# SSM units one tile earlier, RG-LRU scans at tiles 12 and 13, and a second buffer for pair sums in a hybrid recurrent decoder step

## The chip, the cores and the metric

The kernel runs on one core of a Trainium2 chip. The metric is device time in microseconds of one execution; the kernel before takes 869.88 us, the median of three runs (868.09 to 870.44).

## What is computed

One layer of a decoder trunk on 544 tokens (32 of a sample group, 512 of a prompt), in fp32:

```
z = x @ w_in                                  # 1024 -> 6144, split among branches and gates
A: h = RG-LRU scan(conv4(xa)); out_a = (h * gelu(ya)) @ proj_a
B: out_b = (sb * conv3(sc * sh)) @ proj_b
C: y = Re(C state) + D u, a diagonal complex SSM scan over us (32 groups x 64 states)
   zc = gelu(y); out_c = (zc * sigmoid(zc @ glu_w + glu_b)) @ proj_c
m = g0 * out_a + g1 * out_b + g2 * out_c      # g = sigmoid of the last 3072 columns of z
x = LN(ALPHA * x + m @ w_out)
x = LN(ALPHA * x + square(relu(x @ mlp_up)) @ mlp_down)
```

All new states (conv buffers, RG-LRU and SSM states) are outputs too.

## The kernel before, in words

Every large product is made of three matmuls on a high and a low part of each operand (`mm3`, L148): a weight block of 128x1024 comes from DRAM into a `raw` buffer (three of them), ACT rounds it into `wh` and DVE makes `wl = raw - wh`. Four pairs of `wh`/`wl` buffers (five from tile 28 on) stand between these splits and PE. Results go to a ring of four PSUM buffers named `big`; a matmul group on a buffer waits until the group's result of four before has been read out.

The program is written as a row of tiles, numbered by `ti`. Tiles 0 to 7 are the xa and ya columns of z, 8 to 11 sb, 12 to 19 sc and sh in turn (an odd tile ends with the short convolution, a dozen DVE instructions), 20 to 27 the second branch's merge (`merge_b`: 24 pairs of matmuls for the gate and 12 for the projection in each), 28 to 35 the first branch's (`merge7`). The third branch's merge, `w_out` with the first layer norm, the MLP and the second layer norm follow. After each tile `run_side(ti)` calls what was put at that number by `at(...)`.

So the SSM is laid between the tiles. It is cut into eight units of two state groups. For unit u, `ssm_a` (tile `UA[u]`) has PE transpose a small matrix, `ssm_b` (`UB[u]`) makes products whose results DVE multiplies by a rotation (`xx`, `xy`, `X`), scans (L526) and rotates back, POOL joining the two halves of the state `HP`, and `ssm_c` (`UC[u]`) has PE multiply them, the first half at L544 and the second at L545. PE takes its instructions in the order of the program: where `HP` isn't there, PE stands. The RG-LRU's coefficients, scans and outputs (`a_coef`, `a_scan`, `a_first`, `a_out`) are put at tiles in the same way and run on DVE.

A third piece is the paired product `pair7` (L886): seven products in place of eight, on sums of blocks. It needs sums of the weights (`add_pair`: four POOL additions of 128x512 into a buffer `sr`, then split by ACT into `wh` at L851 and by DVE into `wl` at L852) and sums of x (`t_sum`, or `t_make` in the MLP; split by `t_put` into `Tt`, ACT at L790 and DVE at L791). In the MLP `t_make` uses an `sr` buffer of the same pool too, and that pool has one buffer.

The order of instructions of each engine is made by a scheduler, by priorities and estimated costs; what it has put in a row is then executed in that order.

Of the kernel before, what the change touches and what calls it, by code (L numbers as in the profile page):

```python
# [11 lines left out]
F32 = mybir.dt.float32  # L12
# [7 lines left out]
NB, NS = 8, 4  # L20
# [13 lines left out]
RAHEAD = 2  # L34
W2 = 1
AH1 = 4
UA = [12, 14, 16, 18, 20, 22, 23, 25]
UB = [a + 1 for a in UA]
UC = [a + (2 if a > 18 else 3) for a in UA]
K4_FIRST = {"a": (3,), "c": ()}  # L40
# [24 lines left out]
def kernel(ctx: ExitStack, tc: tile.TileContext, I, O):  # L65
# [101 lines left out]
    xh = [stile(F32R, name="xh") for _ in range(2)]  # L167
    xl = [stile(F32R, name="xl") for _ in range(2)]
    cp = const.tile([128, NCP], F32, name="cp")
    gw = const.tile([128, 2, 4, 128], F32, name="gw")  # L170

    def C(n, a=0, b=None):
        o, w = CP[n]
# [199 lines left out]

    def params_af():
        mag, dn, cn, sn = (P[n] for n in ("mag", "dn", "cn", "sn"))
        A_r = const.tile([128, 16, 4], F32, name="A_r")
        A_i = const.tile([128, 16, 4], F32, name="A_i")
        F_r = const.tile([128, 16, 4], F32, name="F_r")
        F_i = const.tile([128, 16, 4], F32, name="F_i")
        u1, u2 = stemp(16), stemp(16)  # L380

        def cmul(orr, oi, ar, ai, br, bi):
            tt(G, u1, ar, br, MUL)
            tt(G, u2, ai, bi, MUL)
            tt(G, orr, u1, u2, SUB)
            tt(G, u1, ar, bi, MUL)
            tt(G, u2, ai, br, MUL)
            tt(G, oi, u1, u2, ADD)

        tt(G, A_r[:, :, 0], mag, cn[:, 0], MUL)  # L390
        tt(G, A_i[:, :, 0], mag, sn[:, 0], MUL)
        cmul(A_r[:, :, 1], A_i[:, :, 1], A_r[:, :, 0], A_i[:, :, 0], A_r[:, :, 0], A_i[:, :, 0])
        cmul(A_r[:, :, 2], A_i[:, :, 2], A_r[:, :, 1], A_i[:, :, 1], A_r[:, :, 0], A_i[:, :, 0])
        cmul(A_r[:, :, 3], A_i[:, :, 3], A_r[:, :, 1], A_i[:, :, 1], A_r[:, :, 1], A_i[:, :, 1])
        rho = ptile(16, "rho")
        tt(G, rho, mag, mag, MUL)
        tt(G, rho, rho, rho, MUL)
        nr = stemp(16)
        ts(G, nr, A_r[:, :, 0], 1.0, None, SUB)
        ni = A_i[:, :, 0]  # L400
        tt(G, u1, nr, C("are"), MUL)
        tt(G, u2, ni, C("aim"), MUL)
        tt(G, u1, u1, u2, ADD)
        tt(G, F_r[:, :, 3], u1, dn, MUL)
        tt(G, u1, ni, C("are"), MUL)
        tt(G, u2, nr, C("aim"), MUL)
        tt(G, u1, u1, u2, SUB)
        tt(G, F_i[:, :, 3], u1, dn, MUL)
        for s in range(3):
            cmul(F_r[:, :, s], F_i[:, :, s], F_r[:, :, 3], F_i[:, :, 3], A_r[:, :, 2 - s], A_i[:, :, 2 - s])  # L410
        P.update(A_r=A_r, A_i=A_i, F_r=F_r, F_i=F_i, rho=rho)
# [27 lines left out]
    MM = [s1.tile([128, 2, 128], F32, tag=f"M{i}", name="M") for i in range(2)]  # L439
    for M_z in MM:  # L440
        G.memset(M_z, 0.0)
    ssr = const.tile([128, 16, NB], F32, name="ssr")
    ssi = const.tile([128, 16, NB], F32, name="ssi")

    def ssm_load(u):
        bc = s1.tile([128, 2, 4, 32], F32, tag="bc", name="bc", bufs=2)
# [230 lines left out]
    side = {}  # L677
# [20 lines left out]
    for ct in range(4):  # L698
        at(2 * ct + 2, a_gate, ct)
        at(2 * ct + 3, a_rec, ct)  # L700
        at(10 + ct, a_coef, ct)
        at(14 + ct, a_scan, ct)
        at(18 + ct, a_out, ct)
    at(0, params_trig)
    at(0, etable)
    at(0, params_af)
    side[9].insert(0, (a_sqrt, ()))
    side[14].insert(0, (a_first, ()))
    at(UB[7], ssm_state)
    at(UC[7], lambda: x_load())  # L710


    ti = 0
# [64 lines left out]

    N1, N2 = slice(0, H2), slice(H2, T)
    X0 = [[t[i] for t in (xh, xl)] for i in range(2)]  # L780
    xq = []

    def x_load():
        for i in range(2):
# [9 lines left out]
    def t_sum(i):  # L794
# [1 line left out]
        d, e = ((a, N1), (a, N2), (b, N2), (b, N1))[i], ((a, N2), (b, N2), (b, N2), (b, N1))[i]  # L796
        f = (d, d, (a, N1), (b, N2))[i]
        d, e, f = (x[:, :, n] for x, n in (d, e, f))
        tt(G if i == 1 else V, d, e, f, SUB)

    def t_next():
        a, b = xq
# [212 lines left out]
    merge_b(bh, bl)  # L1015

    ph1.close()
    srp = ctx.enter_context(tc.tile_pool(name="srp", bufs=1))
    upp = ctx.enter_context(tc.tile_pool(name="upp", bufs=1))
    wst["wp2"] = ctx.enter_context(tc.tile_pool(name="wp2", bufs=W2))  # L1020
    base = cur[0]
# [24 lines left out]
    wq["free"] = [wst["wp2"]] * W2 + [wp] * 4  # L1046
    pump()
    wq["cap"] = 4 + W2
    for i in range(4):
        t_sum(i)  # L1050
    Tt0 = []
    merge7(AQ["ah"], AQ["al"], K4_FIRST["a"], (0,))
    for i in sorted(side):
        run_side(i)
# [448 lines left out]
```

## Time and profile before

| what | value |
| --- | --- |
| median of 3 runs | 869.88 us |
| profiled execution | 870.71 us, of which the span is 868.9 us |
| PE busy | 841.5 us (97%) |
| DVE busy | 621.6 us (72%) |
| ACT busy | 374.0 us (43%) |
| POOL busy | 337.0 us (39%) |

The span runs from the first to the last recorded instruction; the other 1.81 us of that execution lie around it. PE's idle time is 27.4 us, and it lies in few places: 4.6 us at the start, 7.5 us at the end, and the rest in waits that the rows below list.

### The profile page before, as it was taken

How to read it: one execution, taken by the hardware profiler on the slowest of the kernel's cores; microseconds unless marked ns; L12 is line 12 of the kernel's file. 1: busy time of each engine (PE TensorE's matmuls, PEld its weight loads, DVE VectorE, ACT ScalarE, POOL GpSimd, SP SyncE). 2: the span in 40 equal slices, each digit the busy share in tenths (PEclk: the TensorE clock that was granted, in tenths of full speed). 3: DMA queues.
4: the chain of work that ended last, by engine and by line, in shares of the span. 5: the costliest groups of instructions: out<-in, count | busy, mean ns of one | idle time of the engine just before them, and what ended most of it. 6: DMA issues, size and time to landing. Idle time of an engine off the chain costs nothing.

```text
span 868.9 us, 16015 instructions
## 1 busy us (share of the span) xinstructions
PE 841.5 (97%) x6516; PEld 831.0 (96%) x6516; DVE 621.6 (72%) x963; ACT 374.0 (43%) x616; POOL 337.0 (39%) x363
## 2 busy tenths in 40 slices
PE   7999999898999899999999999899999999999996
PEld 7999998898999899999998999899999999999996
DVE  6978969986446766898758787666565666655656
ACT  4453744334432434644437765444343434444310
POOL 1089957777537443633001130422222212122022
PEclk9999999999999999999999999999999999999999
DMA  8352141223125253233754543333232333333202
GB/s 304 120 135 85 50 127 32 80 61 98 34 70 191 71 149 97 73 98 98 249 170 143 160 134 98 112 107 97 79 100 90 98 97 98 98 97 126 93 9 96
DMA packets 31593, 93.99 MB, mean 108 GB/s; under 512 B 3424, under 2 KB 9952, under 8 KB 31136
## 3 DMA queue, kind: packets, MB, share of 16 engines
q1 hardware_dynamic: 31232, 91.92, 33.9%
q8 instruction: 51, 0.84, 0.4%
q0 software_dynamic: 288, 1.05, 0.3%
q14 instruction: 22, 0.18, 0.1%
HBM read 88.24 MB, written 2.49 MB: 104 GB/s over the span
## 4 chain that ended last, share of the span: by engine, by line
PE 78%; DVE 14%; issue 3%; ACT 3%; POOL 1%; DMA 1%; DVEq 0%; SPq 0%; ACTq 0%; POOLq 0%
PE big L148 50%; PE big L886 21%; PE big L1171 3%; DVE wl L117 1%; PE big L1330 1%; DVE Tt L791 1%; DVE X L526 1%; DVE wl L852 1%; DVE cacc L613 1%; DVE xx L240 1%; DVE xy L240 1%; DMA raw<-in_w_dram 1%; ACT wh L851 1%; DVE X L240 1%; PE big L1112 1%
## 5 line engine op out<-in xcount | busy, mean ns | idle before, releaser
L240 POOL TENSOR_TENSOR sr<-raw 128x512 f32<-128x512 f32 x38 | 61.0, 1626 | 242.9 <-DMA raw<-in_w_dram 192.9
L117 DVE TENSOR_TENSOR wl<-raw,wh 128x1024 fp32r<-128x1024 f32 x70 | 96.3, 1379 | 39.4 <-ACT wh L116 39.2
L886 PE MATMUL big<-Tt,wh 128*128 128x272 f32 x608 | 117.7, 290 | 5.7 <-DVE Tt L791 3.0
L148 PE MATMUL big<-xh,wh 128*128 128x272 f32 (+2 forms) x544 | 116.2, 295 | 5.1 <-DVE wh L203 4.6
L116 ACT CAST wh<-raw 128x1024 fp32r<-128x1024 f32 x70 | 73.1, 1048 | 105.5 <-PE big L148 61.1
L148 PE MATMUL big<-xl,wh 128*128 128x272 f32 (+2 forms) x544 | 114.0, 291 | 0.0
L148 PE MATMUL big<-xh,wl 128*128 128x272 f32 (+2 forms) x544 | 113.4, 290 | 0.0
L851 ACT CAST wh<-raw 128x1024 fp32r<-128x1024 f32 (+1 forms) x73 | 68.3, 937 | 94.5 <-PE big L148 49.7
L852 DVE TENSOR_TENSOR wl<-raw,wh 128x1024 fp32r<-128x1024 f32 (+1 forms) x73 | 92.4, 1267 | 17.6 <-ACT wh L851 16.6
L886 PEld LDWEIGHTS big<-Tt,wh 128*128 128x128 f32 x608 | 95.6, 188 | 7.4 <-DVE Tt L791 3.6
L148 PE MATMUL big<-fh,wh 128*128 128x272 f32 (+2 forms) x448 | 98.1, 289 | 0.0
L148 PE MATMUL big<-fh,wl 128*128 128x272 f32 (+2 forms) x448 | 97.9, 288 | 0.0
L148 PE MATMUL big<-fl,wh 128*128 128x272 f32 (+2 forms) x448 | 97.7, 288 | 0.0
L148 PEld LDWEIGHTS big<-xh,wh 128*128 128x128 f32 x544 | 86.5, 192 | 5.7 <-ACT xh L202 4.6
L886 PE MATMUL big<-Tt,wl 128*128 128x272 f32 x304 | 88.0, 290 | 0.8 <-DVE wl L852 0.8
L148 PEld LDWEIGHTS big<-xl,wh 128*128 128x128 f32 x544 | 86.3, 192 | 0.1
L148 PEld LDWEIGHTS big<-xh,wl 128*128 128x128 f32 x544 | 85.7, 191 | 0.0
L851 ACT CAST wh<-sr 128x1024 fp32r<-128x1024 f32 x38 | 39.7, 1046 | 79.7 <-POOL sr L240 60.9
L852 DVE TENSOR_TENSOR wl<-sr,wh 128x1024 fp32r<-128x1024 f32 x38 | 47.9, 1260 | 35.5 <-ACT wh L851 35.5
L148 PEld LDWEIGHTS big<-fh,wh 128*128 128x128 f32 x448 | 72.4, 188 | 0.0
L148 PEld LDWEIGHTS big<-fl,wh 128*128 128x128 f32 x448 | 72.4, 188 | 0.0
L148 PEld LDWEIGHTS big<-fh,wl 128*128 128x128 f32 x448 | 72.0, 189 | 0.0
(291 smaller groups left out, 2093.0 us busy)
## 6 DMA issues: line engine op xcount, KB each, us to landing
raw<-in_w_dram SPq DMA_DIRECT2D x147, 512.0 KB, 3.6
xq<-in_xT_dram SPq DMA_DIRECT2D x2, 1088.0 KB, 7.2
xraw<-in_xT_dram SPq DMA_DIRECT2D x3, 544.0 KB, 7.1
raw<-in_w_dram SPq DMA_DIRECT2D x3, 384.0 KB, 6.2
x<-in_xT_dram SPq DMA_DIRECT2D x2, 576.0 KB, 4.9
U<-us_t SPq DMA_DIRECT2D x16, 68.0 KB, 4.1
zc<-Y SPq DMA_DIRECT2D x16, 68.0 KB, 3.7
bc<-in_bc_dram SPq DMA_DIRECT2D x8, 128.0 KB, 2.2
```

The source lines that it names most:

```text
L116: S.copy(h, r)
L117: V.tensor_tensor(l, r, h.bitcast(F32), op=SUB)
L148: PE.matmul(out, w, x[:, a:b], start=first and oi == 0, stop=last and oi == 2)
L240: e.tensor_tensor(o, a, b, op=op)
L526: V.tensor_tensor_scan(X_[:, r, j], rb, X_[:, r, j], 0.0, op0=MUL, op1=ADD)
L613: V.scalar_tensor_tensor(acc, xp[:, k:568 + k], w(k), acc, op0=MUL, op1=ADD)
L791: V.tensor_tensor(d[:, 1], t, d[:, 0].bitcast(F32), op=SUB)
L851: S.copy(h[:, 0:n], src)
L852: V.tensor_tensor(l[:, 0:n], src, h[:, 0:n].bitcast(F32), op=SUB)
L886: PE.matmul(out, w[:, sl], y[:, k], start=k == 0 and oi == 0, stop=k == 3 and oi == 2)
L1112: PE.transpose(tp[0:n, ft // 4, o:o + 128], x1[ft // 4][:, ft % 4, c0:c1], ident)
L1171: PE.matmul(out, x, w[:, sl], start=first and kk == 0 and oi == 0, stop=kk == K - 1 and oi == 2)
```

## The change

The table `UA` is moved one tile forward, and two for units 5 and 7, and with it `UB` and `UC`: `UC` becomes 14, 16, 18, 20, 21, 22, 24, 25 instead of 15, 17, 19, 21, 22, 24, 25, 27. The coefficients and scans of the RG-LRU go from one channel block per tile (10 to 13, 14 to 17) to two per tile (10 and 11, 12 and 13). The load of x for tile 28's merge follows `UC[7]`; its four sums, which were made just ahead of that merge, are put at tile 26, and one of them goes from POOL to DVE; the first split of them is put at tile 27. The pool of `sr` has two buffers instead of one. Seven tables (`gw`, `A_r`, `A_i`, `F_r`, `F_i`, `ssr` and `ssi`) live in a pool that is given back before tile 28.

```diff
@@ -34,7 +34,7 @@
 RAHEAD = 2
 W2 = 1
 AH1 = 4
-UA = [12, 14, 16, 18, 20, 22, 23, 25]
+UA = [11, 13, 15, 17, 19, 20, 22, 23]
 UB = [a + 1 for a in UA]
 UC = [a + (2 if a > 18 else 3) for a in UA]
 K4_FIRST = {"a": (3,), "c": ()}
@@ -167,7 +167,7 @@
     xh = [stile(F32R, name="xh") for _ in range(2)]
     xl = [stile(F32R, name="xl") for _ in range(2)]
     cp = const.tile([128, NCP], F32, name="cp")
-    gw = const.tile([128, 2, 4, 128], F32, name="gw")
+    gw = s1.tile([128, 2, 4, 128], F32, tag="gw", name="gw")
 
     def C(n, a=0, b=None):
         o, w = CP[n]
@@ -373,10 +373,10 @@
 
     def params_af():
         mag, dn, cn, sn = (P[n] for n in ("mag", "dn", "cn", "sn"))
-        A_r = const.tile([128, 16, 4], F32, name="A_r")
-        A_i = const.tile([128, 16, 4], F32, name="A_i")
-        F_r = const.tile([128, 16, 4], F32, name="F_r")
-        F_i = const.tile([128, 16, 4], F32, name="F_i")
+        A_r = s1.tile([128, 16, 4], F32, tag="A_r", name="A_r")
+        A_i = s1.tile([128, 16, 4], F32, tag="A_i", name="A_i")
+        F_r = s1.tile([128, 16, 4], F32, tag="F_r", name="F_r")
+        F_i = s1.tile([128, 16, 4], F32, tag="F_i", name="F_i")
         u1, u2 = stemp(16), stemp(16)
 
         def cmul(orr, oi, ar, ai, br, bi):
@@ -439,8 +439,8 @@
     MM = [s1.tile([128, 2, 128], F32, tag=f"M{i}", name="M") for i in range(2)]
     for M_z in MM:
         G.memset(M_z, 0.0)
-    ssr = const.tile([128, 16, NB], F32, name="ssr")
-    ssi = const.tile([128, 16, NB], F32, name="ssi")
+    ssr = s1.tile([128, 16, NB], F32, tag="ssr", name="ssr")
+    ssi = s1.tile([128, 16, NB], F32, tag="ssi", name="ssi")
 
     def ssm_load(u):
         bc = s1.tile([128, 2, 4, 32], F32, tag="bc", name="bc", bufs=2)
@@ -698,16 +698,19 @@
     for ct in range(4):
         at(2 * ct + 2, a_gate, ct)
         at(2 * ct + 3, a_rec, ct)
-        at(10 + ct, a_coef, ct)
-        at(14 + ct, a_scan, ct)
+        at(10 + ct // 2, a_coef, ct)
+        at(12 + ct // 2, a_scan, ct)
         at(18 + ct, a_out, ct)
     at(0, params_trig)
     at(0, etable)
     at(0, params_af)
     side[9].insert(0, (a_sqrt, ()))
-    side[14].insert(0, (a_first, ()))
+    side[12].insert(0, (a_first, ()))
     at(UB[7], ssm_state)
     at(UC[7], lambda: x_load())
+    for i in range(4):
+        at(UC[7] + 1, lambda i=i: t_sum(i))
+    at(UC[7] + 2, lambda: t_next())
 
 
     ti = 0
@@ -778,7 +781,7 @@
 
     N1, N2 = slice(0, H2), slice(H2, T)
     X0 = [[t[i] for t in (xh, xl)] for i in range(2)]
-    xq = []
+    xq, Tt0 = [], []
 
     def x_load():
         for i in range(2):
@@ -796,7 +799,7 @@
         d, e = ((a, N1), (a, N2), (b, N2), (b, N1))[i], ((a, N2), (b, N2), (b, N2), (b, N1))[i]
         f = (d, d, (a, N1), (b, N2))[i]
         d, e, f = (x[:, :, n] for x, n in (d, e, f))
-        tt(G if i == 1 else V, d, e, f, SUB)
+        tt(V, d, e, f, SUB)
 
     def t_next():
         a, b = xq
@@ -1015,7 +1018,7 @@
     merge_b(bh, bl)
 
     ph1.close()
-    srp = ctx.enter_context(tc.tile_pool(name="srp", bufs=1))
+    srp = ctx.enter_context(tc.tile_pool(name="srp", bufs=2))
     upp = ctx.enter_context(tc.tile_pool(name="upp", bufs=1))
     wst["wp2"] = ctx.enter_context(tc.tile_pool(name="wp2", bufs=W2))
     base = cur[0]
@@ -1046,9 +1049,6 @@
     wq["free"] = [wst["wp2"]] * W2 + [wp] * 4
     pump()
     wq["cap"] = 4 + W2
-    for i in range(4):
-        t_sum(i)
-    Tt0 = []
     merge7(AQ["ah"], AQ["al"], K4_FIRST["a"], (0,))
     for i in sorted(side):
         run_side(i)
```

Three lines are added to the file, so a line of before such as L791 is L794 after.

DVE at the first SSM unit, before. `xx` and `xy` are the unit's rotations, `X` its scan, `vv` and `bacc` the short convolution, `bx` the RG-LRU scan:

```order
L240 TENSOR_TENSOR xx_1630<-big_1622,E_r_595 128x512
L765 SCALAR_TENSOR_TENSOR bacc_1613<-up_1606,cp_94,bacc_1613 128x560
L240 TENSOR_TENSOR xy_1631<-big_1622,E_i_596 128x512
L767 SCALAR_TENSOR_TENSOR vv_1616<-up_1606,cp_94,bacc_1613 128x32
L769 SCALAR_TENSOR_TENSOR vv_1616<-up_1606,cp_94,bacc_1613 128x512
L240 TENSOR_TENSOR X_1629<-xx_1630,xy_1631 128x256
L240 TENSOR_TENSOR vv_1616<-vv_1616,us_t_159 128x544
L240 TENSOR_TENSOR X_1629<-xx_1630,xy_1631 128x256
L526 SCALAR_TENSOR_TENSOR X_1629<-rho_666,X_1629 128x128 x4
L240 TENSOR_TENSOR tm_1716<-r_841,cp_94 128x32
L665 SCALAR_TENSOR_TENSOR bx_451<-r_841,bx_451 128x512
L240 TENSOR_TENSOR xx_1630<-X_1629,E_r_595 128x512
```

The same place after:

```order
L117 TENSOR_TENSOR wl_1607<-raw_1401,wh_1606 128x1024
L240 TENSOR_TENSOR big_1456<-big_1456,dq_1249 32x64
L240 TENSOR_TENSOR tm_1553<-r_841,cp_94 128x32
L665 SCALAR_TENSOR_TENSOR bx_451<-r_841,bx_451 128x512
L240 TENSOR_TENSOR bx_451<-tm_1553,bx_451 128x4x8
L240 TENSOR_TENSOR tm_1553<-r_841,bx_451 128x32
...
L662 COPY st_96<-bx_451 128x4x8
L240 TENSOR_TENSOR gy_452<-gy_452,bx_451 128x544
L665 SCALAR_TENSOR_TENSOR bx_451<-r_841,bx_451 128x512 x2
L240 TENSOR_TENSOR xx_1573<-big_1565,E_r_595 128x512
L240 TENSOR_TENSOR xy_1574<-big_1565,E_i_596 128x512
```

The RG-LRU's first steps and three of its four scans stood behind the unit's rotations and now stand ahead of them; the convolution stands behind.

DVE at the start of the first branch's merge, before. `Tt` is the split of a sum of x:

```order
L852 TENSOR_TENSOR wl_3506<-raw_3329,wh_3505 128x1024
L791 TENSOR_TENSOR Tt_3509<-xq_3269,Tt_3509 128x1088
L791 TENSOR_TENSOR Tt_3512<-xq_3271,Tt_3512 128x1088
L791 TENSOR_TENSOR Tt_3515<-xq_3269,Tt_3515 128x1088
L852 TENSOR_TENSOR wl_3560<-raw_3501,wh_3559 128x1024
```

And after:

```order
L855 TENSOR_TENSOR wl_3335<-raw_3317,wh_3334 128x1024
L794 TENSOR_TENSOR Tt_3277<-xq_3103,Tt_3277 128x1088
...
L855 TENSOR_TENSOR wl_3509<-raw_3332,wh_3508 128x1024
L794 TENSOR_TENSOR Tt_3512<-xq_3105,Tt_3512 128x1088
L794 TENSOR_TENSOR Tt_3515<-xq_3103,Tt_3515 128x1088
L855 TENSOR_TENSOR wl_3560<-raw_3504,wh_3559 128x1024
```

One of three splits in a row has gone ahead into the tile before.

ACT at the MLP's first paired product, before. `rl` is an output tile of the MLP's upper half leaving PSUM and `fh` its high part; `wh_6234` and `wh_6238` are the splits of the weight's pair sums `sr_6229`, and `sr_6194` is the buffer of `t_make`:

```order
L1226 CAST fh_5763<-rl_6105 128x256
L851 CAST wh_6225<-raw_6211 128x1024
L1224 ACTIVATE rl_6135<-big_6134 128x256
L1226 CAST fh_5763<-rl_6135 128x256
L1224 ACTIVATE rl_6165<-big_6164 128x256
L1226 CAST fh_5763<-rl_6165 128x256
L790 CAST Tt_6196<-sr_6194 128x1088
...
L790 CAST Tt_6208<-sr_6194 128x1088
L851 CAST wh_6234<-sr_6229 128x1024
L851 CAST wh_6238<-sr_6229 128x1024
L851 CAST wh_6294<-raw_6217 128x512
```

And after:

```order
L1226 CAST fh_5763<-rl_6105 128x256
L854 CAST wh_6238<-sr_6229 128x1024
L854 CAST wh_6225<-raw_6211 128x1024
L1224 ACTIVATE rl_6135<-big_6134 128x256
L1226 CAST fh_5763<-rl_6135 128x256
L1224 ACTIVATE rl_6165<-big_6164 128x256
L854 CAST wh_6234<-sr_6229 128x1024
L1226 CAST fh_5763<-rl_6165 128x256
L793 CAST Tt_6196<-sr_6194 128x1088
L793 CAST Tt_6200<-sr_6194 128x1088
L854 CAST wh_6294<-raw_6217 128x512
```

The split `wh_6238` of the pair sums has moved ahead of `wh_6225` and of two evacuations (`rl_6135`, `rl_6165`).

DVE at the same place, before. `x1_5030 <- big_6242` is the evacuation of the first of four tiles of the lower half:

```order
L240 TENSOR_TENSOR fl_5764<-rl_6105,fh_5763 128x256
L852 TENSOR_TENSOR wl_6226<-raw_6211,wh_6225 128x1024
L240 TENSOR_TENSOR rl_6135<-rl_6135 128x256
L240 TENSOR_TENSOR fl_5764<-rl_6135,fh_5763 128x256
L240 TENSOR_TENSOR rl_6165<-rl_6165 128x256
L240 TENSOR_TENSOR fl_5764<-rl_6165,fh_5763 128x256
...
L240 TENSOR_TENSOR sr_6194<-x1_5031,x1_5030 128x1088
L240 TENSOR_TENSOR sr_6194<-x1_5031,sr_6194 128x1088
L1257 SCALAR_TENSOR_TENSOR x1_5030<-x1_5030,big_6242 128x544
L791 TENSOR_TENSOR Tt_6204<-sr_6194,Tt_6204 128x1088
```

And after:

```order
L240 TENSOR_TENSOR fl_5764<-rl_6105,fh_5763 128x256
L855 TENSOR_TENSOR wl_6239<-sr_6229,wh_6238 128x1024
L855 TENSOR_TENSOR wl_6226<-raw_6211,wh_6225 128x1024
...
L240 TENSOR_TENSOR rl_6165<-rl_6165 128x256
L855 TENSOR_TENSOR wl_6235<-sr_6229,wh_6234 128x1024
L240 TENSOR_TENSOR fl_5764<-rl_6165,fh_5763 128x256
L794 TENSOR_TENSOR Tt_6196<-sr_6194,Tt_6196 128x1088
L794 TENSOR_TENSOR Tt_6200<-sr_6194,Tt_6200 128x1088
L240 TENSOR_TENSOR sr_6194<-x1_5031,x1_5030 128x1088
L240 TENSOR_TENSOR sr_6194<-x1_5031,sr_6194 128x1088
L1257 SCALAR_TENSOR_TENSOR x1_5030<-x1_5030,big_6242 128x544
```

Two `wl` splits of the pair sums have moved ahead of the evacuation; by the program's semaphores the first product of `pair7` waits for that evacuation (of `big_6242`), the second for that of `big_6268`, and the third tile of the lower half for ACT's `rl_6135`, in both kernels.

## Rows read from the trace of the kernel before

**Rows 1.** The page's head: busy us (share) xinstructions of each engine.

```profile
PE 841.5 (97%) x6516; PEld 831.0 (96%) x6516; DVE 621.6 (72%) x963; ACT 374.0 (43%) x616; POOL 337.0 (39%) x363
```

**Rows 2.** Waits of PE: engine line <- waited for: us in total, times, longest us.

```profile
PE big L544 <- POOL HP L240: 4.1, 3, 2.2
PE big L545 <- POOL HP L240: 3.6, 3, 1.3
PE big L886 <- DVE Tt L791: 3.0, 3, 1.7
PE big L886 <- ACT wh L851: 1.8, 1, 1.8
PE big L886 <- DVE wl L852: 0.8, 1, 0.8
PE big L886 <- DVE rl L240: 0.7, 1, 0.7
```

**Rows 3.** Timeline of PE: units 0 and 4. start us, us, operation [idle before].

```profile
139.30 0.50 PE L544 MATMUL big<-HP,oo 128*128 128x136 f32 x2 [0.63 <-POOL HP L240]
...
140.96 0.50 PE L545 MATMUL big<-HP,oo 128*128 128x136 f32 x2 [1.16 <-POOL HP L240]
...
212.35 0.50 PE L545 MATMUL big<-HP,oo 128*128 128x136 f32 x2 [1.26 <-POOL HP L240]
```

**Rows 4.** Windows, all engines: us, busy us (x), granted TensorE clock, DMA share, GB/s.

```profile
142.00:144.00 2.00, 2.00 (x11) 2.00 (x11) 1.97 (x4) 1.32 (x2) 1.33 (x2) 0.50 0.50 197
144.00:146.00 2.00, 2.00 (x14) 2.00 (x14) 2.00 (x3) 1.15 (x4) 2.00 (x2) 0.75 0.00 0
162.00:164.00 2.00, 1.86 (x8) 1.86 (x9) 1.97 (x5) 1.33 (x3) 1.97 (x3) 0.52 0.57 180
212.00:214.00 2.00, 1.65 (x11) 1.65 (x12) 0.00 (x0) 0.28 (x1) 0.71 (x3) 0.82 0.83 217
214.00:216.00 2.00, 2.00 (x12) 2.00 (x10) 0.00 (x0) 0.12 (x1) 1.15 (x4) 0.50 0.51 201
218.00:220.00 2.00, 2.00 (x11) 2.00 (x10) 0.00 (x0) 1.17 (x6) 1.69 (x4) 0.50 0.00 0
```

**Rows 5.** One window of DVE, from 114.14 to 208.80.

```profile
114.14:208.80 94.66, 81.01 (x133) 0.96 0.24 74
```

**Rows 6.** Timeline of DVE: unit 0's first product, two RG-LRU scans.

```profile
127.79 0.68 DVE L240 TENSOR_TENSOR xx<-big,E_r 128x512 f32<-128x512 f32 x1
...
142.89 3.13 DVE L665 TENSOR_TENSOR_SCAN bx<-r,bx 128x512 f32<-128x512 f32 x2
```

**Rows 7.** Timeline of POOL: the two halves of unit 4's state.

```profile
208.89 3.40 POOL L240 TENSOR_TENSOR HP<-xx,xy 128x256 f32<-128x256 f32 x2 [2.00 <-DVE xy L240]
```

**Rows 8.** Timeline of DVE: three splits of x at tile 28's merge.

```profile
296.55 7.02 DVE L791 TENSOR_TENSOR Tt<-xq,Tt 128x1088 fp32r<-128x1088 f32 x3
```

**Rows 9.** Timeline of DVE at the MLP's first paired product.

```profile
540.01 0.71 DVE L1257 SCALAR_TENSOR_TENSOR x<-x,big 128x544 f32<-128x544 f32 x1
540.64 2.49 DVE L791 TENSOR_TENSOR Tt<-sr,Tt 128x1088 fp32r<-128x1088 f32 x2
...
548.15 2.58 DVE L852 TENSOR_TENSOR wl<-sr,wh 128x1024 fp32r<-128x1024 f32 x2 [3.13 <-ACT wh L851]
```

**Rows 10.** Timeline of ACT and, below, POOL at the same place.

```profile
547.08 1.04 ACT L851 CAST wh<-sr 128x1024 fp32r<-128x1024 f32 x1 [5.84 <-POOL sr L240]
...
543.27 2.55 POOL L240 TENSOR_TENSOR sr<-raw 128x512 f32<-128x512 f32 x2 [34.00 <-DVE Tt L791]
```

**Rows 11.** Timeline of PE at the same place.

```profile
531.15 0.41 PE L148 MATMUL big<-fh,wh 128*128 128x272 f32 x2
531.40 0.41 PE L148 MATMUL big<-fl,wh 128*128 128x272 f32 x2
...
548.17 0.40 PE L886 MATMUL big<-Tt,wh 128*128 128x272 f32 x1 [1.81 <-ACT wh L851]
```

**Rows 12.** DMA issues at 524.9 to 525.5: KB each, median us to landing.

```profile
raw<-in_w_dram SPq DMA_DIRECT2D x1, 512.0 KB, 5.5
```

## The prediction

> **What bounds the kernel now.** The first view is the head of the page: PE is busy for 841.5 us, 97% of the span of 868.9 [rows 1], so only its 27.4 us of idle time, and time at a lower clock, can be won. Nothing that the change touches makes PE's own list shorter. The second view is the list of PE's waits [rows 2]. Of the waits that the change can reach, the SSM's are the largest: 4.1 and 3.6 us for the state HP in three units (7.7 us), all read by PE in L544 and L545. Next are 3.0 us for the splits Tt of x at the merge that begins at tile 28, and 1.8, 0.8 and 0.7 us (3.3 us) for the pair sums at the MLP's first paired product. The start, the end and two waits of some 1.3 us together stay.
>
> The third view is the granted clock behind the waits [rows 4]. After unit 0's waits it is 0.50 and 0.75 in two windows of 2 us, after unit 1's 0.52 in one, after unit 4's 0.82, 0.50 and 0.50 (with a fourth such window between the two last). So PE, which had been at 2.4 GHz, falls to 1.2 GHz each time after a stretch of short SSM products and waits. Lost time is a window's length times (1 - clock): 1.5 us for unit 0, 1.0 for unit 1 in the window shown, 0.36 + 3 x 1.0 = 3.4 for unit 4. These are 5.9 us; the edges of the falls that the rows leave out bring it to some 6.5. The SSM costs 7.7 + 6.5 = 14.2 us, then, and not only what the list of waits says.
>
> **SSM and RG-LRU: the gain.** What makes HP late is DVE. From 114.14 to 208.80 us, the end of unit 4's last rotation, it is busy for 81.0 of 94.7 us [rows 5]: it waits for 13.7 us in this stretch for things that PE and ACT bring in order, and yet is late at the units. The change lays the scans and the units so that this idle time is filled. Up to the same instruction DVE's new list lacks two splits of the RG-LRU output, one merge instruction and one weight split, by size 2 x 0.9, 0.7 and 1.3 us [rows 9], so 81.0 - 3.8 = 77.2 us. Filled without a gap from 114.1 on it ends at 191.3, and with 1 us for small gaps at 192.3. POOL's two halves of HP took 3.40 us behind it [rows 7]: HP is complete at 194.8 to 195.8.
>
> Would PE be there earlier? It reached unit 4's L545 at 212.35 [rows 3] after 7.7 us of waits and some 2.9 us of lost clock in units 0 and 1, so its work alone would bring it there at 201.75. In the new program the unit's last step stands one merge tile sooner: 36 pairs of matmuls at 0.25 us (one pair starts 0.25 after the other [rows 11]), 9.0 us, so 192.7. HP comes 2.1 to 3.1 us later than that; I take 2.5. This is the sum of all waits up to unit 4, not a wait for each: a unit that stood once starts everything behind it later. At unit 0 I find the first 0.9 us of it. Its rotation xx was at 127.79 [rows 6] and PE's L545 at 140.96 behind 0.63 and 1.16 us of wait [rows 3]. Now some 7.5 us of RG-LRU work stand ahead of xx on DVE (two scans alone are 3.13 us [rows 6]), from 114.1 to 122; the chain from xx to HP loses the 4.2 us of convolution and scan that lay in it, so HP is there at 132 to 134.6, and PE's list, one z tile of 24 pairs (6 us) sooner, reaches it at 133.2.
>
> Waits shrink from 7.7 to 2.5 us. For the clock I take the same proportion, 6.5 to 2.2 (one fall and a part), since no row shows how small a wait must be for no fall. The gain is 14.2 - 4.7 = **9.5 us**. Its ends: 13 us if the waits are 1.2 us and no fall comes, 5 us if three waits of 1 us each bring half of the falls' time and DVE is 1 us later. The x loads and the four sums on DVE (272 x 4 columns each, about twice an evacuation of 0.7 to 1.3 us) come where DVE has spare time, after its last unit; the weight split queued behind them is needed some 9 us later, so I cost them at nothing. If x came more than 9 us late, PE would wait for each us beyond that.
>
> **The splits of x.** Three Tt took 7.02 us in a row [rows 8], 2.34 each, where two elsewhere took 2.49, 1.25 each [rows 9]; POOL was making pair sums beside the first. PE waited three times, 3.0 us, the longest 1.7 [rows 2]. The one split made in tile 27 leaves the second Tt to be the first that PE asks for, no earlier than before: the 1.7 us stay. The two later waits go, as the next product already has its operand. Gain 1.3 us, between 0.5 and 2.5.
>
> The Trainium skill ("GPSIMD Engine Reference", section "8. Key points") says that POOL shares its SBUF interfaces with VectorE and contends with instructions of two SBUF inputs. The 2.34 against 1.25 us agree. By that rule alone DVE's packed stretch could be longer than counted; that is the third rival's ground.
>
> **The second sr buffer: a loss.** Today the pair sums wait for t_make's buffer: POOL starts after 34.00 us of idle time, at 543.27 [rows 10], and PE waits until 548.17 [rows 11]. With two buffers the sums start when their raw block lands. It is issued at 525.0 and takes 5.5 us [rows 12], so 530.5; four additions at 1.28 us [rows 10] end at 535.6. That is 12 us sooner, and the 3.3 us of waits look won. But the scheduler has put their splits ahead on both engines: on ACT wh_6238 stands before wh_6225, rl_6135 and rl_6165, on DVE wl_6239 before eleven instructions, the last of them the evacuation of big_6242. An engine here runs its list in order: in before ACT's last-listed split of a raw block that had landed at 530.5 waited behind the sums too, until after 548 [rows 10]. So both stand from about 530.4 to 535.6, where before they worked.
>
> From 535.6 on: cast 1.04 [rows 10], then on DVE three weight splits, four squares and subtractions of 256 columns (about 0.4 each), two Tt, two sums and the evacuation: 3 x 1.29 + 1.6 + 4 x 1.25 + 0.71 = 11.2 [rows 9], and some 0.5 for ACT's answers. The evacuation ends at 548.4 where it ended at 540.7. PE's list: four lower tiles of 12 pairs from 531.15, 12.0 us, so 543.15. The third of them needs rl_6135, cast + wh_6225 + itself, 538.0, where PE is at 537.15: 0.9 us. Then the first paired product, due at 544.05, waits until 548.4: 4.35 us. It takes 1.6 us (two ran in 543.15 to 546.36); the second needs the next evacuation, two Tt later, 548.4 + 2.5 + 0.7 = 551.6: 1.6 us. After that the splits are long there. Waits 6.85 against 3.3: **3.5 us lost**. The ends: a gain of 3.3 if the order binds less than I read; a loss of 8 if the sums are stretched as Tt was, by 2.34 / 1.25 from 5.1 to 9.6 us, and one of 6.9 if the clock falls once after the longest wait in the kernel's middle, at unit 4's price of 3.4.
>
> **The sum.** 870.71 - 9.5 - 1.3 + 3.5 = 863.4. The profiled execution is 0.83 us above the median of 869.88; against that it would be 862.6. I start from the middle of the two, 870.3, and forecast **863.0**. Its own range, with the SSM between 12 and 7 and the sr buffer between +1 and +6: 858 to 867.
>
> **Rivals.**
> 1. *The pair sums pay as they seem to.* The 3.3 us are won and nothing stands behind them: 870.3 - 9.5 - 1.3 - 3.3 = 856. For it: the sums are 12 us sooner. Against it: the order on two engines. If each instruction could run when its inputs are there, this would be the result. Chance 0.10.
> 2. *The SSM's waits only move.* The RG-LRU burst ahead of unit 0 makes it late by 1.8 us, units 1 and 4 by 1.5 each, and each fall comes back: 4.8 + 6.5 = 11.3, a gain of only 2.9: 870.3 - 2.9 - 1.3 + 3.5 = 869.6. For it: waits of 1.2 us were followed by half clock [rows 3, 4]. Against it: the 13.7 us of idle DVE. Chance 0.18.
> 3. *DVE becomes the bound up to unit 4, slower than before.* Its 77.2 us take longer when POOL works beside them without a pause, as Tt did (2.34 for 1.25). From 114.1 each us more is a us of PE. The kernel breaks even when the SSM loses 14.2 + 1.3 - 3.5 = 12.0 us. With all falls back (6.5) that is 5.5 us of waits, 3.0 more than I count, so DVE's stretch at 80.2 us, 4% longer, is the point from which it is slower; at 82.8, 7%, that can be measured. At 86 us it gives 870.3 + (11.3 + 6.5 - 12.0) = 876. Against it: the 81.0 us of before hold the same contention already. Chance 0.10.
>
> TensorE's clock is a part of each. The Trainium skill ("TensorE: Matmul & The Clock Gate", section "HAM oscillation — how this bites in real kernels") describes how idle PE between groups falls back to half clock, and what that costs. Here the SSM's waits agree [rows 4]; for the 4.35 us wait in the MLP no row shows it, and by that rule 3.4 us would be added, 866.4, within the forecast's own range.
>
> **How the numbers follow.** Forecast 0.62, rivals 0.10, 0.18 and 0.10. A measurement of this kernel can tell 0.3%, 2.6 us, from no change. Faster, below 867.3: the forecast and rival 1, 0.72. Within 0.3%: rival 2, 0.18. Slower: rival 3, 0.10. The range that leaves out rival 3 and the lower half of rival 1 is 856.5 to 869.5.
>
> **What would show it.** In the profile after, PE's waits for HP sum to 2 to 3 us before unit 4 and one fall of the clock at most stays there; DVE has no idle time over 1 us from 114 to 192; one wait for Tt of about 1.7 us is left at tile 28's merge; POOL's pair sums for the MLP start near 520 (530.5 less the gains before them) and end 5 us later; ACT and DVE stand idle for 5 us ahead of them, and PE waits over 4 us at the first paired product of the MLP. If this wait is missing, rival 1 is right there; if the sum of HP waits is over 4 us, rival 2 or 3.

## The result

| | before | after |
| --- | --- | --- |
| median (4 runs each) | 870.16 us | 875.95 us (874.72 to 877.41) |
| ratio | | 1.0072, interval 1.005 to 1.0095 |
| profiled execution, its span | 870.71, 868.9 us | 877.41, 875.6 us |

The change makes the kernel slower by 0.72%, some 6 us. The forecast was 863.0, and the range ended at 869.5. (The kernel before has one run more here than above. Ratios here and below are taken from all runs and can differ a little from the quotient of two medians.) The head of the page after answers to [rows 1]:

```profile
PE 843.5 (96%) x6516; PEld 832.2 (95%) x6516; DVE 630.6 (72%) x964; ACT 374.1 (43%) x616; POOL 333.7 (38%) x362
```

PE's idle time is 875.6 - 843.5 = 32.1 us, where it was 27.4; its busy time is 2.0 us longer. The list of PE's waits answers to [rows 2]:

```profile
PE big L889 <- DVE x L1257: 4.1, 2, 3.9
PE big L544 <- POOL HP L240: 3.3, 2, 3.0
PE big L545 <- POOL HP L240: 2.7, 3, 1.2
PE big L490 <- POOL wt L240: 2.5, 2, 1.6
PE big L148 <- ACT M L502: 2.3, 3, 0.8
PE big L889 <- DVE Tt L794: 1.8, 1, 1.8
PE big L889 <- DVE rl L240: 1.1, 1, 1.1
...
PE big L148 <- ACT rl L1224: 0.4, 1, 0.4
PE big L148 <- ACT th L963: 0.4, 1, 0.4
```

The waits in the SSM's stretch are those for HP (3.3 and 2.7), wt (2.5), M (2.3) and th (0.4): 11.2 us, where it was 7.7 us for HP alone. (Of a unit, wt is a table that POOL makes and M a matrix that ACT copies; th belongs to the gate of the second branch's merge.) The three waits for Tt have become one, 3.0 to 1.8, but a wait of 1.1 for rl is new. The 3.3 us for the pair sums have become 4.1 + 0.4 for evacuations. In all 3.5 - 1.2 + 1.1 + 1.2 = 4.6 us more, the difference in idle time but for a rounding. The timeline of PE shows where the large ones lie (start, busy us, operation, idle time before it):

```profile
187.52 0.50 PE L545 MATMUL big<-HP,oo 128*128 128x136 f32 x2 [0.27 <-POOL HP L240]
...
190.47 0.41 PE L490 MATMUL big<-ident,wt 128*128 128x128 f32 x2 [0.82 <-POOL wt L240]
...
192.53 0.44 PE L490 MATMUL big<-ident,wt 128*128 128x128 f32 x2 [1.65 <-POOL wt L240]
...
208.16 0.82 PE L544 MATMUL big<-HP,oo 128*128 128x136 f32 x2 [3.00 <-POOL HP L240]
...
302.60 0.39 PE L889 MATMUL big<-Tt,wh 128*128 128x272 f32 x1 [1.77 <-DVE Tt L794]
...
350.32 0.52 PE L889 MATMUL big<-Tt,wh 128*128 128x272 f32 x2 [1.05 <-DVE rl L240]
...
552.11 0.39 PE L889 MATMUL big<-x1h,wh 128*128 128x272 f32 x1 [3.92 <-DVE x L1257]
```

The wait for rl at 350.32 is not one for the splits of x: a weight split that stands ahead of rl on DVE took 2.27 us, beside POOL's additions, where before it took 1.32 (at 347.29 and 344.23).

Two rows tell in which stage the 6.7 us between the two profiles were lost. They are the first paired product of tile 28's merge, before and after:

```profile
293.64 0.29 PE L886 MATMUL big<-xh,wh 128*128 128x272 f32 x1
```

```profile
297.26 0.29 PE L889 MATMUL big<-xh,wh 128*128 128x272 f32 x1
```

PE starts the MLP's lower half at 535.30, where it did at 531.15 [rows 11]. So 3.6 us were lost up to tile 28, where 9.5 us were to be won, 0.5 us from there to the MLP's lower half, and 2.6 us from there to the end.

Up to unit 3 it went somewhat better than before: PE multiplied its state at 187.52 after a wait of 0.27, where before it did so at 198.11; of these 10.6 us 9.0 are the merge tile by which the step stands sooner. Then PE waits for unit 5's wt (190.47, 192.53), and 3.00 us for unit 4's HP (208.16). The windows of all engines answer to [rows 4] (us, busy us of PE, PEld, DVE, ACT and POOL, granted clock, DMA share, GB/s):

```profile
194.00:196.00 2.00, 1.78 (x8) 1.79 (x9) 2.00 (x3) 1.08 (x5) 1.91 (x3) 0.51 0.00 0
208.00:210.00 2.00, 1.84 (x7) 1.67 (x8) 0.00 (x0) 0.00 (x0) 0.97 (x3) 0.50 0.53 207
210.00:212.00 2.00, 2.00 (x11) 2.00 (x11) 0.00 (x0) 0.40 (x1) 0.90 (x2) 0.50 0.00 0
212.00:214.00 2.00, 2.00 (x11) 2.00 (x11) 0.80 (x2) 0.79 (x3) 1.92 (x6) 0.50 0.00 0
304.00:306.00 2.00, 2.00 (x11) 2.00 (x10) 2.00 (x2) 1.10 (x1) 2.00 (x1) 0.50 0.00 0
552.00:554.00 2.00, 1.90 (x9) 1.90 (x10) 2.00 (x3) 1.50 (x2) 0.00 (x0) 0.61 0.03 8
554.00:556.00 2.00, 1.79 (x9) 1.47 (x8) 2.00 (x4) 0.39 (x1) 0.00 (x0) 0.53 0.00 0
```

No fall of the clock is left behind units 0 to 3. But it falls to 1.2 GHz behind the wait for wt, behind the one for HP, and, which it had not done before, behind the wait of 1.77 us for Tt and behind the 3.92 us in the MLP. By these windows 1.0 us is lost at 194, 3.0 at 208 to 214, 1.0 at 304 and 0.8 + 0.9 at 552 to 556, and somewhat more in windows at the edges of the first three.

Why unit 4 came late is seen on DVE and POOL. The stretch of [rows 5], from 114.14 to the end of unit 4's last rotation, for all engines after (DVE is the third, POOL the fifth):

```profile
114.14:203.50 89.36, 81.05 (x632) 78.92 (x631) 84.57 (x131) 38.59 (x113) 71.31 (x92) 0.98 0.24 75
```

The same of the kernel before:

```profile
114.14:208.80 94.66, 89.46 (x698) 88.65 (x697) 81.01 (x133) 38.28 (x106) 69.68 (x88) 0.96 0.24 74
```

DVE is busy for 84.57 us, where its list at the durations of before makes 77; the lists differ by few instructions, 131 against 133 shown. The timeline of DVE shows the rest of the delay:

```profile
118.64 0.22 DVE L240 TENSOR_TENSOR tm<-r,cp 128x32 f32<-128x32 f32 x1 [3.63 <-ACT r L651]
...
196.06 0.69 DVE L240 TENSOR_TENSOR xx<-big,E_r 128x512 f32<-128x512 f32 x1
...
202.27 1.23 DVE L240 TENSOR_TENSOR xy<-X,E_i 128x512 f32<-128x512 f32 x1
```

DVE stood for 3.63 us at 118.64 for ACT's `r`, the coefficients of the scans that had been put ahead; from then on it never stood for longer than 0.04 us. Before, it had stood as long at that place (3.64 us, for a weight) and three times more, for 4.99, 2.88 and 1.48 us; only these three are filled. Unit 4's products were done by PE at 189.65, and their rotation xx started at 196.06, behind the convolution, the splits `al` and `bl` and a weight split. The last rotation ended at 203.50. POOL, at that time:

```profile
187.92 1.68 POOL L240 TENSOR_TENSOR wt<-F_r,bc 128x256 f32<-128x256 f32 x2
...
191.38 1.09 POOL L240 TENSOR_TENSOR wt<-wt,sp 128x256 f32<-128x256 f32 x1
...
204.05 1.09 POOL L240 TENSOR_TENSOR wt<-wt,sp 128x256 f32<-128x256 f32 x1
...
207.38 1.40 POOL L240 TENSOR_TENSOR HP<-xx,xy 128x256 f32<-128x256 f32 x2
```

POOL was in unit 5's wt until 192.5 while PE waited for it, and had taken up unit 6's tables when unit 4's rotation came at 203.50: HP started at 207.38, 3.9 us later, and was complete 5.3 us behind the rotation, where before it took 3.40 [rows 7].

At the MLP, one line of POOL and two of DVE answer to [rows 9, 10]:

```profile
534.28 2.65 POOL L240 TENSOR_TENSOR sr<-raw 128x512 f32<-128x512 f32 x2 [20.89 <-DMA raw<-in_w_dram]
```

```profile
540.66 1.22 DVE L855 TENSOR_TENSOR wl<-sr,wh 128x1024 fp32r<-128x1024 f32 x1 [6.11 <-ACT wh L854]
...
551.34 0.71 DVE L1257 SCALAR_TENSOR_TENSOR x<-x,big 128x544 f32<-128x544 f32 x1
```

The sums start when the block lands, 9 us sooner than before, and DVE stands for 6.11 us ahead of their split; the evacuation for which PE waits ends at 552.05, where before it ended at 540.7.

### The profile page after: what moved, and what is told of

It is laid out like the page before. It is cut to its first block, busy times and chain, and to the rows that moved or that the text cites. A ratio compares the mean times of both kernels' runs of the same rounds, so it can differ in the third digit from the quotient of the medians.

```text
span 875.6 us, 16024 instructions
## 1 busy us (share of the span) xinstructions
PE 843.5 (96%) x6516; PEld 832.2 (95%) x6516; DVE 630.6 (72%) x964; ACT 374.1 (43%) x616; POOL 333.7 (38%) x362
## 4 chain that ended last, share of the span: by engine, by line
PE 76%; DVE 12%; ACT 4%; POOL 3%; issue 3%; DMA 1%; DVEq 0%; SPq 0%; ACTq 0%; POOLq 0%
PE big L148 48%; PE big L889 21%; PE big L1171 3%; PE big L1330 1%; DVE wl L117 1%; DVE wl L855 1%; DVE X L526 1%; DVE cacc L613 1%; DMA raw<-in_w_dram 1%; ACT M L502 1%; POOL wt L240 1%; DVE Tt L794 1%; DVE bx L240 1%; DVE xx L240 1%; ACT wh L116 1%
## 5 line engine op out<-in xcount | busy, mean ns | idle before, releaser
L855 DVE TENSOR_TENSOR wl<-raw,wh 128x1024 fp32r<-128x1024 f32 (+1 forms) x73 | 95.3, 1305 | 21.9 <-ACT wh L854 21.0
```

Source lines behind the costliest of these rows:

```text
L855: V.tensor_tensor(l[:, 0:n], src, h[:, 0:n].bitcast(F32), op=SUB)
```

## Experiments

Ratios are against the kernel before on the same chip; the changed kernel's is 1.0072 (1.0050 to 1.0095).

**One sr buffer.** The changed kernel with

```diff
-    srp = ctx.enter_context(tc.tile_pool(name="srp", bufs=2))
+    srp = ctx.enter_context(tc.tile_pool(name="srp", bufs=1))
```

> The changed kernel with one sr buffer in place of two. Theory: with two, the splits of the pair sums stand ahead of PSUM evacuations in the rows of ACT and DVE, and cost 4.6 us of waits and one fall of the clock (1.7 us) where 3.3 us were to be won; so with one buffer it is 2.9 us faster than the changed kernel, near 873, with waits of 1.8, 0.8 and 0.7 us for the pair sums and no wait for an evacuation of the lower half. Rival: the waits come from work that is late for another reason; then it stays near 876 and the wait of 3.9 us stays.

Measured: 873.38, ratio 1.0053 (1.0035 to 1.0070), so 0.19% or 1.7 us better than the changed kernel. Waits of PE:

```profile
PE big L889 <- ACT wh L854: 1.8, 1, 1.8
PE big L889 <- DVE wl L855: 0.8, 1, 0.8
```

The waits for the evacuation are gone and the old 1.8 and 0.8 are back, as expected; the gain is smaller than the 2.9 us expected, and the two intervals overlap. Its profile shows why it can be smaller: here the clock falls behind the old waits too, which it had not done in the profile before. It is 0.58, 0.50, 0.50 and 0.72 in the four windows of 2 us from 550 on, so 3.4 us are lost, against 1.7 in the changed kernel. The next run is the other test of the price.

**Two sr buffers alone.** The kernel before with `bufs=2` and the seven tables moved (as in the diff of the change).

> The kernel before with two sr buffers and the seven tables moved to make room, all else as before. Theory of the held queues: 3.5 us slower than before as worked out, 2.9 as the changed kernel's trace shows: 873, with a wait of about 4 us for the evacuation of the lower half's first tile and a fall of the clock behind it. Rival (the second buffer pays, the loss belongs to other parts): 3 us faster than before, 867.

Measured: 871.68, ratio 1.0035 (1.0017 to 1.0052): 3.0 us slower. Waits of PE:

```profile
PE big L886 <- DVE x L1257: 3.9, 1, 3.9
...
PE big L148 <- ACT rl L1224: 0.8, 1, 0.8
```

The second buffer costs about what the working gave (3.5 us) and what the changed kernel's trace shows (2.6 us from the lower half to the end). The rival falls. The moved tables are in this run too; no run has them alone.

**Unit 5 one tile later.** The changed kernel with

```diff
-UA = [11, 13, 15, 17, 19, 20, 22, 23]
+UA = [11, 13, 15, 17, 19, 21, 22, 23]
```

> The changed kernel with SSM unit 5 one tile later (products at tile 21, result at 23), units 0 to 4 and 6, 7 as changed. Theory: unit 5 follows unit 4 by one tile, about 9 us of PE, while POOL needs some 15 us for a unit; so PE waits 2.5 us for wt, 0.4 for the gate's th, 3.0 for HP, and the clock falls twice (1.7 and 3.4 us), 11 us in all. One tile later the 2.5 and the first fall go, and some or all of the rest: 5 to 11 us faster than the changed kernel, 865 to 871. Rival (the scans put ahead of unit 0 make DVE late for all units): the waits stay, within 2 us of 876.

Measured: 875.29, ratio 1.0072 (1.0044 to 1.0099): nothing gained. My first theory fell, and with it a misreading: the wait of 3.0 us for HP belongs to unit 4, not 5. The waits for wt did go, but PE then came sooner to unit 4's HP and waited longer there:

```profile
204.22 0.82 PE L544 MATMUL big<-HP,oo 128*128 128x136 f32 x2 [4.84 <-POOL HP L240]
```

DVE's last rotation of that unit still ended only at 202.4. So POOL's wt is not the bound here: DVE's list ends later, and a wait that is taken away ahead of it comes back.

**The scans back at their old tiles.** The changed kernel with

```diff
-        at(10 + ct // 2, a_coef, ct)
-        at(12 + ct // 2, a_scan, ct)
+        at(10 + ct, a_coef, ct)
+        at(14 + ct, a_scan, ct)
-    side[12].insert(0, (a_first, ()))
+    side[14].insert(0, (a_first, ()))
```

> The changed kernel with the RG-LRU coefficients and scans back at one channel block per tile (10 to 13, 14 to 17), all else as changed. Theory of unit 5: the waits of unit 5 stay, only those of units 0 to 2 change, by less than 3 us either way: 873 to 879. Rival (the two scans per tile are what makes the SSM late): HP and wt waits of unit 5 shrink too and the kernel is 3 us or more faster than the changed one.

Measured: 875.30, ratio 1.0076 (1.0046 to 1.0106), the same as the changed kernel. PE waits 6.1 us at L544 and 0.5 at L545 for HP, and 2.5 for wt: the sum is again 9 us, at other units. The burst of scans, the second rival's ground, is not what makes it late.

**Half of POOL's SSM work, in the changed kernel and in the one before.** In both, `ssm_lin` leaves out two of its three instructions, so the output is not the layer's:

```diff
-        t = s1.tile(sh, F32, tag="sp", name="sp")
         for d, p, q, op in terms:
             tt(G, d, x(p[0]), x(p[1]), MUL)
-            tt(G, t, x(q[0]), x(q[1]), MUL)
-            tt(G, d, d, t, op)
```

> The changed kernel with POOL's SSM tables cut to the first of three instructions (the second product and the sum are left out of wt and oo), so its output is not the layer's; DVE's list and order up to unit 4 are the same. Theory of contention: DVE's stretch from 114 to unit 4's last rotation was 84.6 us busy where the same instructions at their durations before would make 77; with half of POOL's work gone it falls to 77 or less, and the kernel is 6 us or more faster than the changed one. Rival (the order alone makes DVE late): the stretch stays within 2 us of 84.6 and only the waits for wt go (2.5 us and a fall, 4 us).

> The kernel before with the same cut of POOL's work, as the control; its output is not the layer's either. Theory of contention: DVE's 81.0 us from 114 to unit 4's end fall too, by 3 us or more, and HP's waits shrink from 7.7 to 4 us or less: 864 to 867. Rival (order alone): DVE's stretch stays within 2 us of 81 and the waits stay.

Measured: 858.54, ratio 0.9872 (0.9849 to 0.9895), and 861.75, ratio 0.9904 (0.9881 to 0.9928). Against the changed kernel the first is 2%, 17 us, faster; no wait for HP, wt or M is left in its list, and PE is at the second half of unit 4's state at 193.45, where the prediction had it at 192.7 if it waits for nothing. The DVE stretch up to unit 4's last rotation, first of the changed kernel so lightened, then of the kernel before:

```profile
114.14:188.64 74.50, 74.50 (x613) 74.50 (x613) 67.65 (x131) 37.17 (x111) 38.32 (x52) 1.00 0.26 83
```

```profile
114.14:203.56 89.42, 86.67 (x684) 86.15 (x683) 70.18 (x133) 37.33 (x105) 35.11 (x48) 0.96 0.23 73
```

The same 131 instructions in the same order, but for two memsets one place apart, take DVE 67.65 us where they took 84.57, when POOL works for 38.32 us instead of 71.31. In the kernel before, it is 70.18 instead of 81.01. One form shows it best, the SSM's scan on DVE between 114 and 204, in the changed kernel and in the lighter one (busy us, mean ns):

```profile
L526 DVE TENSOR_TENSOR_SCAN X<-rho,X 128x128 f32<-128x128 f32 x20 | 12.3, 676 | 0.0
```

```profile
L523 DVE TENSOR_TENSOR_SCAN X<-rho,X 128x128 f32<-128x128 f32 x24 | 8.2, 402 | 0.0
```

676 ns against 402 for the same tile; in the kernel before it was 568. The mean is a mix. The changed kernel's own trace has unit 0's four scans, beside which POOL ran nothing, and unit 1's four; the last row is the second of three POOL products beside unit 1's:

```profile
129.29 1.37 DVE L526 TENSOR_TENSOR_SCAN X<-rho,X 128x128 f32<-128x128 f32 x4
147.21 2.66 DVE L526 TENSOR_TENSOR_SCAN X<-rho,X 128x128 f32<-128x128 f32 x4
```

```profile
147.84 0.74 POOL L240 TENSOR_TENSOR oo<-oo,sp 128x256 f32<-128x256 f32 x1
```

Unit 0's took 400 to 418 ns each; of unit 1's the three that met a product took 774 to 892 and the last, with POOL idle, 393. Of the 20 scans in the stretch 13 took 768 ns or more, in the kernel before 8 of 20, in the lighter one none. All these 21 started while a POOL product ran, and none of the other 19 of the two kernels did. The rotations xx that read a product from PSUM took 677 to 693 ns in all four kernels. So a DVE instruction with both inputs in SBUF can get longer where it meets one of POOL: this is contention. By these runs each us of POOL work costs DVE (84.57 - 67.65) / (71.31 - 38.32) = 0.51 us in the changed kernel and (81.01 - 70.18) / (69.68 - 35.11) = 0.31 in the one before. That DVE idled more before is only a part of this difference: added up from the rows of both engines, POOL worked beside a busy DVE for 67.0 of its 71.3 us after and for 60.3 of 69.7 before. The rest is which instructions meet, as the scans show. And with POOL's load halved the changed kernel is 3.2 us faster than the one before, second sr buffer and all: the earlier units do pay when DVE has the time.

**The units alone.** The kernel before with the new `UA` and nothing else.

> The kernel before with the table of SSM units alone changed, to the odd tiles. Theory (units closer together keep POOL busy, and with it each DVE instruction of the SSM and the convolution takes longer, so DVE is the bound): slower than before by 3 to 9 us, 873 to 879, with waits for HP, wt and M of 10 us or more. Rival (the earlier units alone are good, only the scans ahead of them hurt): faster than before.

Measured: 873.85, ratio 1.0050 (1.0034 to 1.0065), 4.3 us slower. Waits of PE:

```profile
PE big L544 <- POOL HP L240: 5.9, 2, 3.0
...
PE big L490 <- POOL wt L240: 2.5, 2, 1.6
...
PE big L148 <- ACT M L502: 0.8, 1, 0.8
...
PE big L545 <- POOL HP L240: 0.4, 2, 0.2
```

9.6 us of waits for HP, wt and M where there were 7.7, at other units: slower as the theory has it, with waits a little under the 10 us expected, and the rival falls. Not all of the 4.3 us need lie in the SSM: in this profile PE is at tile 28's first product at 295.12, 1.5 us later than before, and the rest is lost behind, where the clock falls at waits at which it hadn't in the profile before. But the sign is the same in every profile: with the units moved forward and all of POOL's work PE is there between 295.1 and 297.9 (six kernels), with units and scans as before between 290.2 and 293.6 (three).

**Even tiles, and sooner still.** To tell the odd tile from the packing, with scans and sums as changed and one sr buffer:

```diff
-UA = [11, 13, 15, 17, 19, 20, 22, 23]
+UA = [10, 12, 14, 16, 18, 20, 22, 23]
```

> As the run with scans and sums moved, with the first five SSM units two tiles sooner on even tiles (10, 12, 14, 16, 18), the others at 20, 22, 23. It tells the odd tile from the closeness: if the rotation standing behind the short convolution of an odd tile is what hurts, HP waits stay under 4 us and it is faster than before by 0.7% or more; if the packing of POOL and DVE is what hurts, the waits are 8 us or more and it is within 0.3% of before or slower.

Measured: 874.62, ratio 1.0064 (1.0042 to 1.0086). The largest waits:

```profile
PE big L544 <- POOL HP L240: 5.1, 3, 3.3
...
PE big L490 <- POOL wt L240: 1.5, 1, 1.5
```

With HP's other 1.6, 1.2 for M and 0.7 more it is 10 us. Being on an odd tile is not the cause. That the packing is, this run only allows: the first five units are two tiles apart as before, but lie further ahead, in the shorter z tiles.

**The scans alone.** The kernel before with the coefficients at `10 + ct // 2` and the scans at `12 + ct // 2`.

> The kernel before with the RG-LRU coefficients and scans alone moved (two channel blocks per tile: 10 and 11, 12 and 13). Theory (DVE is the bound of the SSM, and the units on odd tiles are what set its rotations behind the short convolution): with the units where they were, the scans fill the 8.6 us that DVE idles before 125, so the waits for HP of units 0 and 1 (1.8 and 3.4 us) shrink: 2 to 6 us faster than before, 864 to 868 where before is 870. Rival (the burst of scans is itself what makes the changed kernel late): 2 us or more slower than before.

Measured: 865.70, ratio 0.9955 (0.9936 to 0.9974), 3.9 us faster. The waits for HP, 7.7 us before, are

```profile
PE big L544 <- POOL HP L240: 3.7, 4, 1.5
PE big L545 <- POOL HP L240: 1.8, 4, 1.3
```

5.5 us. That is in the range expected. With the units where they were, the scans moved ahead pay; with the units moved they bring nothing.

**The sums of x alone.** The kernel before with the load at tile 25, the four sums at 26, the first split at 27, all on DVE, and the seven tables moved.

> The kernel before with x loaded at tile 25, its sums made at 26 on DVE and the first split at 27, and the seven tables moved; SSM, RG-LRU and the sr buffer as before. Theory: two of the three waits for Tt (1.25 us) go and nothing else: 1 us faster than before, within what can be measured. Rival: the clock falls behind the one longer wait as in the changed kernel's trace (1.7 us), or the sums delay weight splits; then the same as before or 1 us slower.

Measured: 867.20, ratio 0.9967 (0.9949 to 0.9985), 2.9 us faster where I expected 1. One wait for Tt of 1.8 us is left, as worked out. Where the other 1.6 us are from isn't settled. In its profile no fall of the clock follows unit 4, and PE is at tile 28's first product at 290.16, 3.5 us sooner than before, which is ahead of the waits for Tt; but the moved tables are in this run too.

**Scans and sums together.** The two edits in one kernel, units and sr buffer as before.

> The kernel before with the scans moved (as in the run with them alone, 0.45% faster) and the sums of x made at tile 26 on DVE (0.33% faster alone); SSM units and the sr buffer as before. The parts lie 80 us apart, so they should add: 0.7 to 0.9% faster than before, 862.5 to 864 where before is 870. Rival (their gains are partly the clock's, which falls here or there): half of it, 0.4%.

Measured: 863.94, ratio 0.9950 (0.9933 to 0.9966): 0.50% faster than the kernel before, near the rival's half and not the sum of the parts. It has the lowest median of the kernels that compute the layer, but its interval holds the ratio of the scans alone (0.9955) too, so what the sums add to them is not shown.

**Two sr buffers, ACT's splits held back.** The version above with `bufs=2` and, for the two splits of the pair sums, `pin(S.copy(h, src))`, by which they keep their place in the program on ACT.

> As the run with scans and sums moved, with two sr buffers and ACT's splits of the pair sums kept in program order, by which they stand behind the first PSUM evacuation on ACT instead of ahead of it, but on DVE still ahead of the lower half's first evacuation. Theory of the held queues: the wait for that evacuation falls from 3.9 to about 3 us and no wait for the splits is left, so within 1.5 us of the run with one buffer. Rival (any second buffer costs the 3 us): 3 us slower than it.

Measured: 866.27, ratio 0.9954 (0.9936 to 0.9973), by ratio the same as with one buffer, though the medians lie 2.3 us apart. Waits of PE:

```profile
PE big L889 <- DVE x L1257: 3.2, 2, 1.9
```

With the first evacuation ahead of the splits on ACT no loss of 3 us is seen any more. A wait of 3.2 us for the lower half is left, where DVE still does the splits first; it is a little longer than the waits of 1.8 and 0.8 us for the sums that it replaces.

## Why the prediction was wrong, step by step

- **DVE's stretch, the step that failed.** "So 81.0 - 3.8 = 77.2 us" took the durations of before, as if they held for any order. Packed, the list took 84.57, 7.4 more. Of this 6.1 are contention: the half of POOL's work that the two lighter runs leave out cost DVE 81.01 - 70.18 = 10.8 us before and 84.57 - 67.65 = 16.9 after. The other 1.3 are that the two lists, so relieved, differ by 2.5 us and not 3.8. And 1 us was allowed for gaps, where 4.8 came, 3.63 of them for ACT's `r`: the coefficients had been moved with the scans, and ACT makes them. Unit 4's last rotation ended at 203.5 instead of 191.3 to 192.3.
- **The third rival was right** in place and mechanism, with a chance of 0.10; the sum of HP waits, 6.0 us, is over the 4 us named as its sign. It put the point from which it can be measured at a stretch of 82.8 us; the stretch was 84.6, for which its rule gives 870.3 + (7.4 + 2.5 + 6.5 - 12.0) = 874.7, and the time was 875.95. In part this nearness is luck: it has every fall of the SSM back, where two went and one came, and counts fewer waits than came. "Against it: the 81.0 us of before hold the same contention already" was the reasoning that failed: they hold contention, but less of it, 10.8 us against 16.9 by the same runs. The Trainium skill ("GPSIMD Engine Reference", section "8. Key points") has the rule that POOL contends with VectorE instructions of two SBUF inputs, which I set behind this rival; the traces agree, with 676 against 402 ns.
- **PE's way to unit 4.** Its work was counted nearly right (192.7 against 193.45 in the lighter kernel, without waits). All waits up to and with unit 4 were counted as 2.5 us. For HP alone they were 6.0, half of them at unit 4; and 2.5 us for wt, 2.3 for M and 0.4 for th were in no step. Unit 5 had been put one tile behind unit 4, some 9 us, and POOL makes one unit's tables after the other; M waits for an addition on DVE that stands behind other work.
- **The clock.** "One fall and a part", 2.2 us, in the SSM: the falls behind units 0 and 1 did go. Two came, at wt and at unit 4's HP, 1.0 and 3.0 us in the windows shown, where before 5.9 were lost. Then there were two that no step had: behind the Tt wait, which was 1.7 us and without a fall before, and behind the MLP's 3.92 us. The price of this last was the 1.7 us of the two windows shown, not 3.4. The Trainium skill ("TensorE: Matmul & The Clock Gate", section "HAM oscillation — how this bites in real kernels") says that PE which idles between groups falls back to half clock; the MLP's windows agree, with 0.61 and 0.53 behind the 3.92 us.
- **The splits of x.** Two of three waits went, 1.2 us, as worked out (1.3). The fall behind the third, 1.0 us in the window shown, was in no step; nor was the wait of 1.1 us for rl, which is contention too and not a price of this edit.
- **The second sr buffer.** "3.5 us lost": alone it measured 3.0. The evacuation was put 12.8 us after the end of the sums (548.4 - 535.6) and came 12.5 after (552.05 - 539.54); the wait at the first product was put at 4.35 and was 3.92. This step was right in mechanism. That the size came out is in part luck: waits of 6.85 us were counted and 4.5 came, as the second evacuation took 0.2 instead of 1.6 and rl_6135 0.4 instead of 0.9, and the fall of the clock, which was left out, made up for it.
- **The sum.** With -9.5 replaced by the 3.6 us lost up to tile 28 in the two profiles, the steps give 870.3 + 3.6 - 1.3 + 3.5 = 876.1, and with the +4.3 that the units alone measured 876.8, both near the 875.95. With all three parts as measured alone (+4.3, -2.9 and +3.0) it is 874.7. The scans' 3.9 us, which they gain with the old units, are in the changed kernel worth nothing. The forecast's own range adds up to 868 at its upper end, not 867, with 7 and +6; this changes nothing here.

What stays open: how the 17 us of the lighter kernel divide between DVE's shorter instructions and POOL's own lists coming in time. The DVE stretch shows the first, and leaving POOL's work out does both. What the moved tables do by themselves is open too.

## What to carry to other kernels

Idle time of an engine is not room at the price of the busy time: before a stretch is packed, its instructions are to be priced at what they take while the neighbour engine works beside them, as POOL did beside DVE here, and a run with that neighbour's work cut gives this price directly. When a wait is taken away ahead of a later bound, as wt's was, it comes back there, so the engine whose list ends last is the one to shorten. A second buffer lets work start sooner, but look in the rows of each engine at what has been put ahead of what: a split that stands waiting ahead of a PSUM evacuation costs more than the wait that it was to remove.

## What the hardware showed that I had not expected

- A DVE scan of 128x128 took some 400 ns or some 770 to 960, by whether a POOL product was running when it started; the mean of 676 is of neither kind. POOL pays as well: of unit 2's two halves of HP one took 0.74 us and the other, ahead of which a weight split had begun on DVE by 0.01 us, 1.79.
- The clock fell behind one wait of 1.77 us in the changed kernel, with 0.50 from 304 to 306, and did not behind the same wait of 1.74 us in the profile before.
- The falls differ between executions of one kernel: in the twelve of the version with scans and sums the mean granted clock lay between 0.986 and 0.997 and the time between 870.09 and 862.58, the highest clock with the shortest time. The profile of that version is the slowest of the twelve, 6.1 us above its median.
